# Two transformer blocks on one core: block 2's token factor moves from h to the products, and the norms' sums are issued later

## Chip, cores and metric

One core of a Trainium2 chip runs the whole kernel. The metric is the device time of one execution in microseconds (us); lower is better.

## What is computed

The input x has 512 tokens of 1024 features. It goes through a first block of two layers and then a second block of two layers. Each layer is a mixer and a feed-forward part (ffn), each with a norm ahead of it and a norm behind it. Cut to what matters here:

```python
def rms_norm_2(x, gain):
    xf = x.astype(jnp.float32)
    y = xf * lax.rsqrt(jnp.mean(xf * xf, axis=-1, keepdims=True) + RMS_EPS)
    return y.astype(x.dtype) * gain

def second_block(x, positions, ...):
    for l in range(DEPTH):
        h = rms_norm_2(x, g_pre_mix[l])
        m = hybrid_mixer_2(h, positions, w_in[l], ...)
        x = x + rms_norm_2(m, g_post_mix[l])
        h = rms_norm_2(x, g_pre_ffn[l])
        f = conv_ffn(h, w_up[l], conv_w[l], conv_b[l], w_down[l])
        x = x + rms_norm_2(f, g_post_ffn[l])
    return x
```

The first block has the same frame, but its h is `rms_norm(x) * (1 + sc) + sh`: a shift is added after the norm. In the second block the mixer begins with `h @ w_in`, which yields rotated queries and keys, values, gates and the inputs of a second attention (`sb`); the ffn is `h @ w_up`, a causal convolution over three tokens, gelu times a linear part, and `@ w_down`. In both, the reciprocal root of a token's mean square is one factor per token, so it commutes with the matrix product over features.

## The kernel before

**Layout.** Activations lie feature-major: eight tiles (KT = 8) of 128 features x 512 tokens. Every operand of a matmul is split into a high and a low part, and `mm3` (L314) makes one product of 128 features from three matmuls: hi by hi, hi by lo, lo by hi. So a tile of 128 outputs by 512 tokens takes 24 matmuls, and one over half of the tokens 24 shorter ones.

**Weights.** `load` (L257) brings a chunk by DMA into `raw`, ScalarE copies it into `whi` (L265), VectorE, or GpSimd where the caller says so, subtracts for `wlo` (L267). Four pairs of `whi` and `wlo` exist; a copy waits until TensorE has let go of a pair.

**A joint.** The last tiles of a part are made by `out_proj` (mixer) and `down2` (ffn): one tile `op` after the other, the last ones in two halves of 256 tokens by `in_halves` (L343): all items for the first half, then all in reverse order for the second. Behind the last of the first half stands the post-norm (L476: the sum of squares of y as a matmul with ones into `nrm`, then Ln and Exp for `rstd`, then for each of eight tiles `yn` at L488 and the x add at L489), and behind it the pre-norm (L437): squares of x on ScalarE (L444), adds in pairs on VectorE (L446), four matmuls into `nrm`, `rstd`, and per tile `xn` (L458), `hh` (L460, L462) and `hl` (L468, L473). `norms` (L362) says at which item of the second half each of these is issued: the post-norm at item 0, the pre-norm at item LA or LB. The second half's post-norm comes when all items are done, and its pre-norm (`pending`) is issued by `fm_split` (L377) of the next part. That makes the first tiles of the next part, over the first half of the tokens tile by tile and then over the second in reverse order; `pending` stands before the tile with number LC (ffn) or LD (mixer). The mixer makes some values (`values_steps`) between the halves.

**Order of work.** Each engine runs its instructions in the order in which a list scheduler wrote them down when the kernel was built, from the order of issue in the code and its waits; nothing is reordered when it runs, and the instruction at the head holds up what stands behind it.

**Block 2's users of h.** `mix2` takes rotated parts by `rope` (L568), copies for the compressed values (`vc`), query and key products by `sb_proj` (L1485), the merge gates by `sigmoid`, and values by `values_steps` and `ev_v`; the ffn's `conv` (L1536) reads a finished tile from its bank three times.

Of the kernel before, what the change touches and what calls it, by code (L numbers as in the profile page):

```python
# [10 lines left out]
F32 = mybir.dt.float32  # L11
# [3 lines left out]
ALU = mybir.AluOpType  # L15
# [3 lines left out]
P = 128  # L19
# [24 lines left out]
PH2 = 0  # L44
PXM = 0
SA = 0
LA = 2
# [3 lines left out]
LB = 1  # L51
LC = 4
LD = 2
# [133 lines left out]
class Net:  # L187
    def __init__(self, ctx, tc, A, out):
# [10 lines left out]
        self.pending = lambda: None  # L199
# [162 lines left out]
    def norms(self, y, sqs, g, nxt, late):  # L362
# [13 lines left out]
    def fm_split(self, chunks, act, pool, more=None):  # L376
# [60 lines left out]
    def pre_norm(self, hs, gs, sh, hh, hl):  # L437
# [4 lines left out]
        for k in range(KT):  # L442
# [6 lines left out]
            if sq is None:  # L449
                self.matmul(ps[:, :256], self.ones, s2, start=k == min(1, PAIRS), stop=k == KT - 1)  # L450
        r = self.half("rstd")
        self.ln_exp_rstd(ps[:, :256], r, D)
        ts = []
        for k in range(KT + LAG):
            if k < KT:
# [3 lines left out]
                if sh is None:  # L459
                    nc.scalar.activation(hh[k][:, hs], t, AF.Copy)  # L460
                else:
                    nc.scalar.activation(hh[k][:, hs], t, AF.Identity, bias=sh[:, k:k + 1])  # L462
            if k >= LAG:
                j = k - LAG
                lo, hi = hl[j][:, hs], hh[j][:, hs].bitcast(F32)
                pool = (PH2 if sh is None else PH1) >> j & 1
                if sh is None:
                    (nc.gpsimd if pool else nc.vector).tensor_tensor(lo, ts[j], hi, ALU.subtract)  # L468
                elif pool:
# [5 lines left out]
    def post_norm(self, hs, y, sqs, g, end=False):  # L475
# [1260 lines left out]
```

## Time and profile before

| | |
|---|---|
| median of 3 runs | 3232.23 us (3228.86 to 3241.45) |
| the profiled execution, own time | 3238.15 us |
| its span, first to last instruction | 3236.2 us |
| mean granted TensorE clock | 0.975 |
| TensorE busy | 3060.6 us (95%) |
| VectorE busy | 1958.9 us (61%) |
| ScalarE busy | 1552.1 us (48%) |

[...] A busy TensorE at half clock takes about twice as long for a matmul. A row of waits names who waited, what for, and how long altogether, how often, and at most. The seven joints lie, by the time since the start of the span, at 380 to 425 (block 1 layer 0, mixer to ffn), 755 to 830 (ffn to layer 1's mixer), 1125 to 1195 (layer 1, mixer to ffn), 1505 to 1575 (into block 2), 1975 to 2045, 2355 to 2425 and 2825 to 2885 (the same three places in block 2).

### The profile page before, as it was taken

What the parts mean: (1) busy time and instruction counts of PE and PEld (TensorE: products, weight loads), DVE (VectorE), ACT (ScalarE), POOL (GpSimd) and SP (SyncE); (2) the same over time, 40 slices, a digit from 0 to 9 for tenths busy, and PEclk for the clock granted to TensorE, in tenths of its full rate; (3) what the DMA queues carried; (4) which work ended last, traced back from release to release, by engine and by line L of the source; (5) the groups of instructions that cost most, each with busy time, mean ns of one, the idle gap of its engine ahead of it and who ended that gap; (6) DMA issues with size and microseconds to landing.
All of it is one profiled execution on the core that took longest, in us unless ns stands there. A gap on an engine that the chain in (4) does not pass through costs nothing.

```text
span 3236.2 us, 42643 instructions
## 1 busy us (share of the span) xinstructions
PE 3060.6 (95%) x16196; PEld 2552.1 (79%) x16196; DVE 1958.9 (61%) x3542; ACT 1552.1 (48%) x2768; POOL 338.4 (10%) x329
## 2 busy tenths in 40 slices
PE   6898899998999899999999998999989999999998
PEld 5674787887875688888988778888888878788887
DVE  6778575546477463235677676645566766676365
ACT  4445642234444652224477665534445866454343
POOL 4352000001442000000100111000002001200000
PEclk8899999998998999999999999999999999999999
DMA  7235365644322232323421123323243112332323
GB/s 229 82 109 197 99 215 188 214 130 149 102 89 78 72 114 83 112 86 112 150 76 40 57 68 133 115 91 104 85 158 115 40 46 72 111 118 84 112 86 107
DMA packets 118925, 358.40 MB, mean 111 GB/s; under 512 B 15408, under 2 KB 28464, under 8 KB 118720
## 3 DMA queue, kind: packets, MB, share of 16 engines
q1 hardware_dynamic: 118720, 355.68, 34.2%
q8 instruction: 127, 2.08, 0.3%
q14 instruction: 78, 0.64, 0.1%
HBM read 336.19 MB, written 8.42 MB: 106 GB/s over the span
## 4 chain that ended last, share of the span: by engine, by line
PE 69%; DVE 10%; issue 10%; ACT 5%; DMA 3%; POOL 2%; SPq 0%; POOLq 0%; DVEq 0%; ACTq 0%
PE ps L305 26%; PE op L305 12%; PE pj L305 11%; PE dn L305 7%; PE tk L305 4%; PE nrm L305 2%; PE po L305 2%; DMA wm<-in_w_mod_dram 2%; DVE wlo L267 1%; DVE yn L488 1%; PE pt L308 1%; DVE x L489 1%; POOL mg L1357 1%; ACT whi L265 1%; DVE wm L633 1%
## 5 line engine op out<-in xcount | busy, mean ns | idle before, releaser
L265 ACT ACTIVATE whi<-raw 128x1024 fp32r<-128x1024 f32 (+1 forms) x562 | 550.0, 980 | 812.1 <-PE ps L305 204.0
L267 DVE TENSOR_TENSOR wlo<-raw,whi 128x1024 fp32r<-128x1024 f32 x500 | 559.1, 1122 | 530.5 <-ACT whi L265 527.4
L305 PE MATMUL ps<-hh,whi 128*128 128x512 f32 (+1 forms) x1560 | 574.4, 368 | 0.0
L305 PE MATMUL ps<-hl,whi 128*128 128x512 f32 (+1 forms) x1560 | 572.9, 367 | 0.0
L305 PE MATMUL ps<-hh,wlo 128*128 128x512 f32 (+1 forms) x1560 | 572.7, 367 | 0.0
L305 PE MATMUL pj<-hh,whi 128*128 128x512 f32 (+1 forms) x944 | 357.0, 379 | 23.5 <-ACT hh L654 13.3
L305 PE MATMUL pj<-hl,whi 128*128 128x512 f32 (+1 forms) x944 | 354.2, 375 | 4.4 <-POOL hl L656 4.4
L305 PE MATMUL pj<-hh,wlo 128*128 128x512 f32 (+1 forms) x944 | 352.1, 373 | 0.0
L305 PEld LDWEIGHTS ps<-hh,whi 128*128 128x128 f32 x1560 | 295.4, 189 | 48.1
L305 PEld LDWEIGHTS ps<-hh,wlo 128*128 128x128 f32 x1560 | 295.2, 189 | 48.3
L305 PEld LDWEIGHTS ps<-hl,whi 128*128 128x128 f32 x1560 | 295.5, 189 | 47.9
L305 PEld LDWEIGHTS pj<-hh,whi 128*128 128x128 f32 x944 | 181.5, 193 | 65.9 <-ACT hh L654 15.7
L305 PEld LDWEIGHTS pj<-hl,whi 128*128 128x128 f32 x944 | 181.9, 193 | 35.4 <-POOL hl L656 6.6
L305 PEld LDWEIGHTS pj<-hh,wlo 128*128 128x128 f32 x944 | 181.6, 192 | 30.2 <-issue 1.0
L633 DVE CUSTOM_DVE_ANT_0 wm<-wm,cact 128x1024 f32<-128x1024 f32 x96 | 121.6, 1270 | 112.1 <-DMA wm<-in_w_mod_dram 110.2
L267 POOL TENSOR_TENSOR wlo<-raw,whi 128x1024 fp32r<-128x1024 f32 x62 | 153.5, 2491 | 285.3 <-ACT whi L265 180.2
L305 PE MATMUL op<-hidh,whi 128*128 128x256 f32 (+1 forms) x572 | 178.9, 313 | 0.0
L305 PE MATMUL op<-hidh,wlo 128*128 128x256 f32 (+1 forms) x572 | 177.4, 310 | 0.3 <-DVE wlo L267 0.3
L305 PE MATMUL op<-hidl,whi 128*128 128x256 f32 (+1 forms) x572 | 176.9, 309 | 0.0
L575 POOL TENSOR_TENSOR rp<-rp,rp 128x512 f32<-128x512 f32 (+1 forms) x20 | 28.7, 1437 | 1091.7 <-DVE rp L574 1002.5
L305 PE MATMUL dn<-hidh,whi 128*128 128x512 f32 x352 | 137.8, 391 | 2.3 <-ACT hidh L254 2.3
L305 PE MATMUL dn<-hidl,whi 128*128 128x512 f32 x352 | 137.6, 391 | 0.2 <-DVE hidl L255 0.2
(352 smaller groups left out, 6151.4 us busy)
## 6 DMA issues: line engine op xcount, KB each, us to landing
raw<-in_w_in_dram SPq DMA_DIRECT2D x134, 512.0 KB, 3.4
raw<-in_w_up_dram SPq DMA_DIRECT2D x100, 512.0 KB, 3.5
wm<-in_w_mod_dram SPq DMA_DIRECT2D x96, 512.0 KB, 4.4
raw<-in_w_gu_dram SPq DMA_DIRECT2D x94, 512.0 KB, 3.4
raw<-in_w_dn_dram SPq DMA_DIRECT2D x80, 512.0 KB, 3.5
raw<-in_w_out_dram SPq DMA_DIRECT2D x52, 512.0 KB, 3.5
raw<-in_w_dn_dram SPq DMA_DIRECT2D x80, 192.0 KB, 3.1
hp<-rp SPq DMA_DIRECT2D x96, 64.0 KB, 2.0
```

The lines of the kernel that those rows point to most:

```text
L265: nc_.scalar.activation(hi[:, :n], raw[:, :n], AF.Copy)
L267: (self.lo_eng or nc_.vector).tensor_tensor(lo[:, :n], raw[:, :n], hi[:, :n].bitcast(F32), ALU.subtract)
L305: return self.paced(self.nc.tensor.matmul(*args, **kw))
L308: return self.paced(self.nc.tensor.transpose(*args))
L488: nc.vector.scalar_tensor_tensor(t, y(k, hs), g[:, k:k + 1], r, ALU.mult, ALU.mult)
L489: (nc.gpsimd if PXM >> k & 1 else nc.vector).tensor_tensor(self.x[k][:, hs], self.x[k][:, hs], t, ALU.add)
L575: nc.gpsimd.tensor_tensor(t1[r], t1[r], t2[r], ALU.subtract)
L633: self.nc.vector.tensor_tensor_reduce(raw, raw, self.cact, 1.0, 0.0, ALU.mult, ALU.add, self.mod[l][:, c:c + 1])
L1357: nc.gpsimd.tensor_tensor(s, s, gate[1, f], ALU.add)
```

## The change

In block 2 h becomes x times the gain alone (`raw_h`). The token factor `r2` is computed beside (`token_norm`) and multiplied into what is made of the products: into the rope tables (`cosr`, `sinr`), `vc`, the gates before their sigmoid, `sb_proj`, the values by columns of r2 (`columns`, `split_by`) and each ffn tile ahead of its convolution. In both blocks the post-norm of the second half is issued inside `fm_split`, after eight products of its first tile group; the pre-norm of the first half is issued at item 4 (mixer) or 3 (ffn) instead of 2 or 1, in block 2 at the last item; the pre-norm of the second half is issued after five tiles' worth of products, in block 2's ffn later still, in a mixer between the halves. `fm_split` takes its tiles in groups of four (KG), feature tile by feature tile (`k`) across the group. The DMAs that spill x follow the second post-norm.

```diff
-LA = 2
+LA = 4
...
-LB = 1
-LC = 4
-LD = 2
+LB = 3
+LC = 5
+KG = 4
...
+    def split_by(self, src, f, hi, lo):
+
+        self.nc.scalar.activation(hi, src, AF.Copy, scale=f)
+        self.nc.vector.scalar_tensor_tensor(lo, src, f, hi.bitcast(F32), ALU.mult, ALU.subtract)
...
-        post = [lambda i=i: self.post_norm(HALVES[i], y, sqs, g) for i in range(2)]
-        pre = [lambda i=i: self.pre_norm(HALVES[i], *nxt, *h) for i in range(2)]
-        self.pending = pre[1]
-        if late == 0:
-            return {0: lambda: (post[0](), pre[0]())}, post[1], h
-        return {0: post[0], late: pre[0]}, post[1], h
+        gs, sh = nxt
+        post = [lambda i=i: self.post_norm(HALVES[i], y, sqs, g, pool=0 if sh is None else PXM) for i in range(2)]
+        if sh is None:
+            self.r2 = r2 = self.unit("r2")
+            make = [lambda i=i: self.raw_h(HALVES[i], gs, *h) for i in range(2)]
+            pre = [lambda i=i: self.token_norm(HALVES[i], r2) for i in range(2)]
+            post = [lambda i=i, p=p: (p(), make[i]()) for i, p in enumerate(post)]
+        else:
+            pre = [lambda i=i: self.pre_norm(HALVES[i], gs, sh, *h) for i in range(2)]
+        self.pending = post[1], pre[1], sh is None
+        return {0: post[0], last if sh is None else late: pre[0]}, lambda: None, h
...
-        begin = {LC if more is None else LD: self.pending}
-        middle = {} if more is None else {0: lambda: run(steps(more, 4))}
-        self.in_halves([(i, [src]) for i, src in enumerate(chunks)], KF if more is None else KM,
-                       lambda i, ws, hs, _: self.fm(tiles[i], ws[0], 0, act, hs, range(KT)), pool,
-                       begin, middle)
+        n, keep = len(chunks), KF if more is None else KM
+        late = None if more is not None else (n + 2) * KT if self.pending[2] else LC * KT
+        kept, loads, count = {}, 0, 0
+        ah, al = act
+        for hs in HALVES:
+            first = hs is HALVES[0]
+            if not first and more is not None:
+                run(steps(more, 2))
+                self.pending[1]()
+                if self.pending[2]:
+                    run(steps(more, 2))
+            order = list(range(n)) if first else list(range(n))[::-1]
+            for o in range(0, n, KG):
+                group = []
+                for i in order[o:o + KG]:
...
+                    group.append((i, ws))
+                for k in range(KT):
+                    c = slice(k * P, k * P + P)
+                    for i, (hi, lo) in group:
+                        if count == KT:
+                            self.pending[0]()
+                            if spill:
+                                self.spill()
+                        if count == late:
+                            self.pending[1]()
+                        count += 1
+                        self.mm3(tiles[i][:, hs], hi[:, c], lo[:, c], ah(k, hs), al(k, hs), k == 0, k == KT - 1)
...
+    def raw_h(self, hs, gs, hh, hl):
+
+        nc, x = self.nc, self.x
+        for k in range(KT):
+            nc.scalar.activation(hh[k][:, hs], x[k][:, hs], AF.Copy, scale=gs[:, k:k + 1])
+            nc.vector.scalar_tensor_tensor(hl[k][:, hs], x[k][:, hs], gs[:, k:k + 1], hh[k][:, hs].bitcast(F32), ALU.mult, ALU.subtract)
+
+    def token_norm(self, hs, r2):
+
+        self.ln_exp_rstd(self.squares(hs)[:, :256], r2[:, hs], D)
...
+        tabs = [self.unit(s) for s in ("cosr", "sinr")]
+        for t, o in zip(tabs, (self.cos, self.sin)):
+            nc.vector.tensor_tensor(t, o, r2, ALU.mult)
...
-            nc.scalar.activation(vc[g][0:64], pss[2 + g][64:128], AF.Copy)
-            nc.scalar.activation(vc[g][64:128, 0:T - 1], pss[2 + g][64:128, 1:T], AF.Copy)
+            nc.vector.tensor_tensor(vc[g][64:128], pss[2 + g][64:128], r2[64:128], ALU.mult)
+            nc.scalar.activation(vc[g][0:64], vc[g][64:128], AF.Copy)
+            nc.vector.tensor_tensor(vc[g][64:128, 0:T - 1], pss[2 + g][64:128, 1:T], r2[64:128, 1:T], ALU.mult)
...
-                self.sigmoid(t, ps)
+                nc.vector.tensor_tensor(t, ps, r2, ALU.mult)
+                self.sigmoid(t, t)
...
-            self.nc.scalar.activation(hi, ps, AF.Copy, scale=sc)
-            self.nc.vector.scalar_tensor_tensor(lo, ps, sc, hi.bitcast(F32), ALU.mult, ALU.subtract)
+            t = self.unit("sbt")
+            self.nc.vector.scalar_tensor_tensor(t, ps, (0.125, 1.0)[i], self.r2, ALU.mult, ALU.mult)
+            self.split(t, hi, lo)
...
-                nc.scalar.activation(c, ps, AF.Identity, bias=par[:, b:b + 1], scale=w(2))
+                nc.vector.tensor_tensor(v, ps, r2, ALU.mult)
+                nc.scalar.activation(c, v, AF.Identity, bias=par[:, b:b + 1], scale=w(2))
                 for j in (1, 0):
                     s = 2 - j
-                    nc.vector.scalar_tensor_tensor(c[:, s:], ps[:, :T - s], w(j), c[:, s:], ALU.mult, ALU.add)
+                    nc.vector.scalar_tensor_tensor(c[:, s:], v[:, :T - s], w(j), c[:, s:], ALU.mult, ALU.add)
```

How the rows of VectorE move is told by three places. The first is the joint at 380 to 425, first half: `sq` are the adds of squares that TensorE's sums wait for, `wlo` the conversions of weights. Before:

```order
L508 TENSOR_TENSOR ssy_637_3132<-ssy_637_3132,sqy_712_3498 128x256
L267 TENSOR_TENSOR wlo_745_3662<-raw_743_3660,whi_744_3661 128x1024
L508 TENSOR_TENSOR ssy_637_3132<-ssy_637_3132,sqy_714_3527 128x256
L446 TENSOR_TENSOR sq_717_3533<-sq_716_3531,sq_717_3533 128x256
L446 TENSOR_TENSOR sq_719_3539<-sq_718_3537,sq_719_3539 128x256
L446 TENSOR_TENSOR sq_721_3545<-sq_720_3543,sq_721_3545 128x256
```

And with the change, after the same `ssy` adds:

```order
L271 TENSOR_TENSOR wlo_750_3697<-raw_748_3695,whi_749_3696 128x1024
L271 TENSOR_TENSOR wlo_755_3732<-raw_753_3730,whi_754_3731 128x1024
L563 TENSOR_TENSOR ssy_637_3132<-ssy_637_3132,sqy_719_3562 128x256
L271 TENSOR_TENSOR wlo_773_3780<-raw_771_3778,whi_772_3779 128x1024
L563 TENSOR_TENSOR ssy_637_3132<-ssy_637_3132,sqy_724_3597 128x256
L490 TENSOR_TENSOR sq_727_3603<-sq_726_3601,sq_727_3603 128x256
L490 TENSOR_TENSOR sq_729_3609<-sq_728_3607,sq_729_3609 128x256
```

The adds of squares stand two tiles later, behind three more conversions, the last of them that of a weight of the next part.

The second place is the joint at 1125 to 1195, where the rope tables of block 2 (`ang`, `n`, `r`) are computed beside the post-norm's second half (`yn`). Before:

```order
L508 TENSOR_TENSOR ssy_1878_9742<-ssy_1878_9742,sqy_1988_10302 128x256
L508 TENSOR_TENSOR ssy_1878_9742<-ssy_1878_9742,sqy_1993_10337 128x256
L267 TENSOR_TENSOR wlo_2041_10539<-raw_2039_10537,whi_2040_10538 128x1024
L488 SCALAR_TENSOR_TENSOR yn_2000_10379<-y_1870_9734,mod1_122,rstd_1999_10376 128x256
L488 SCALAR_TENSOR_TENSOR yn_2001_10382<-y_1871_9735,mod1_122,rstd_1999_10376 128x256
```

With the change:

```order
L619 TENSOR_SCALAR r_2003_10385<-r_2003_10385 128x512
L614 SCALAR_TENSOR_TENSOR r_2005_10396<-n_2004_10392,ang_2001_10378 128x512
L271 TENSOR_TENSOR wlo_2044_10571<-raw_2042_10569,whi_2043_10570 128x1024
L615 SCALAR_TENSOR_TENSOR r_2005_10396<-n_2004_10392,r_2005_10396 128x512
L271 TENSOR_TENSOR wlo_2047_10577<-raw_2045_10575,whi_2046_10576 128x1024
L616 SCALAR_TENSOR_TENSOR r_2005_10396<-n_2004_10392,r_2005_10396 128x512
L271 TENSOR_TENSOR wlo_2068_10691<-raw_2066_10689,whi_2067_10690 128x1024
L618 TENSOR_SCALAR r_2005_10396<-r_2005_10396 128x512
L619 TENSOR_SCALAR r_2005_10396<-r_2005_10396 128x512
L543 SCALAR_TENSOR_TENSOR yn_2034_10473<-y_1870_9735,mod1_122,rstd_2033_10469 128x256
```

All of the tables' operations now stand ahead of `yn`, and three conversions among them.

The third place is the joint at 1975 to 2045, first half, from the last x add on. Before:

```order
L489 TENSOR_TENSOR x_3339_18085<-x_3339_18085,yn_3399_18380 128x256
L508 TENSOR_TENSOR ssy_3326_18043<-ssy_3326_18043,sqy_3401_18409 128x256
L267 TENSOR_TENSOR wlo_3434_18573<-raw_3432_18571,whi_3433_18572 128x1024
L508 TENSOR_TENSOR ssy_3326_18043<-ssy_3326_18043,sqy_3403_18438 128x256
L446 TENSOR_TENSOR sq_3406_18444<-sq_3405_18442,sq_3406_18444 128x256
```

With the change:

```order
L544 TENSOR_TENSOR x_3335_18103<-x_3335_18103,yn_3396_18399 128x256
L271 TENSOR_TENSOR wlo_3413_18548<-raw_3411_18546,whi_3412_18547 128x1024
L502 SCALAR_TENSOR_TENSOR hl_3344_18120<-x_3328_18096,par2_0_111,hh_3336_18112 128x256
L271 TENSOR_TENSOR wlo_3418_18583<-raw_3416_18581,whi_3417_18582 128x1024
L502 SCALAR_TENSOR_TENSOR hl_3345_18121<-x_3329_18097,par2_0_111,hh_3337_18113 128x256
L271 TENSOR_TENSOR wlo_3432_18645<-raw_3430_18643,whi_3431_18644 128x1024
L502 SCALAR_TENSOR_TENSOR hl_3346_18122<-x_3330_18098,par2_0_111,hh_3338_18114 128x256
```

The `hl` follow the x adds at once, conversions between them, and the squares come after.

## Rows read from the trace of the kernel before

**Rows 1.** Page, part 1: busy us of each engine, share of the span, instructions.

```profile
PE 3060.6 (95%) x16196; PEld 2552.1 (79%) x16196; DVE 1958.9 (61%) x3542; ACT 1552.1 (48%) x2768; POOL 338.4 (10%) x329
```

**Rows 2.** Stretches: length; busy us of PE, PEld, DVE, ACT, POOL; clock; DMA share; GB/s.

```profile
380.00:425.00 45.00, 41.25 (x314) 39.87 (x313) 38.59 (x82) 28.93 (x63) 0.00 (x0) 0.96 0.36 117
755.00:830.00 75.00, 59.34 (x414) 56.80 (x413) 45.64 (x87) 34.31 (x66) 22.04 (x9) 0.86 0.38 122
1125.00:1195.00 70.00, 59.10 (x431) 56.62 (x430) 51.70 (x103) 37.93 (x71) 0.00 (x0) 0.90 0.33 105
1505.00:1575.00 70.00, 61.08 (x438) 58.64 (x437) 48.26 (x102) 33.16 (x67) 0.00 (x0) 0.90 0.45 144
1975.00:2045.00 70.00, 66.09 (x514) 64.14 (x513) 47.77 (x97) 37.06 (x77) 0.00 (x0) 0.98 0.34 114
2355.00:2425.00 70.00, 61.07 (x466) 59.14 (x465) 49.53 (x104) 33.85 (x67) 0.00 (x0) 0.95 0.47 155
2825.00:2885.00 60.00, 56.25 (x431) 54.35 (x431) 43.33 (x92) 33.12 (x71) 0.00 (x0) 0.97 0.32 106
1575.00:1975.00 400.00, 385.83 (x2112) 319.54 (x2111) 268.47 (x562) 255.87 (x548) 50.77 (x73) 0.99 0.24 77
2045.00:2355.00 310.00, 310.00 (x1452) 260.28 (x1452) 171.51 (x215) 130.25 (x174) 0.00 (x0) 1.00 0.31 99
```

**Rows 3.** TensorE's waits by joint: 380:425 (as 2825), 755:830 (two), 1125, 1505 (as 2355), 1975.

```profile
PE nrm L305 <- DVE sq L446: 3.7, 1, 3.7
...
PE nrm L305 <- DVE sq L446: 11.9, 2, 6.1
...
PE nrm L305 <- DVE ssy L1087: 3.8, 1, 3.8
...
PE nrm L305 <- DVE sq L446: 10.9, 2, 7.1
...
PE nrm L305 <- DVE sq L446: 8.9, 2, 5.8
...
PE nrm L305 <- DVE sq L446: 3.9, 2, 3.7
```

**Rows 4.** TensorE's waits from 1575 to 1975, the mixer's products.

```profile
PE pj L305 <- DVE mg L1324: 3.1, 5, 1.2
...
PE pj L305 <- ACT mg L275: 1.8, 1, 1.8
```

**Rows 5.** VectorE in order of time: start, us, operation, idle before.

```profile
1983.94 0.88 DVE L488 SCALAR_TENSOR_TENSOR yn<-y,par,rstd 128x256 f32<-128x256 f32 x2 [4.17 <-ACT rstd L275]
...
1989.13 0.76 DVE L489 TENSOR_TENSOR x<-x,yn 128x256 f32<-128x256 f32 x2
...
1996.44 1.67 DVE L458 SCALAR_TENSOR_TENSOR xn<-x,par,rstd 128x256 f32<-128x256 f32 x4 [2.27 <-ACT rstd L275]
```

**Rows 6.** Groups by line: a weight's copy (1560 to 2045) and its conversion (2045 to 2355).

```profile
L265 ACT ACTIVATE whi<-raw 128x1024 fp32r<-128x1024 f32 x65 | 68.6, 1056 | 59.7 <-PE pj L305 28.4 <-PE op L305 13.1 <-PE ps L305 11.3
...
L267 DVE TENSOR_TENSOR wlo<-raw,whi 128x1024 fp32r<-128x1024 f32 x53 | 65.0, 1226 | 109.9 <-ACT whi L265 109.9
```

**Rows 7.** GpSimd's conversions from 755 to 830, and VectorE at 797.39.

```profile
L267 POOL TENSOR_TENSOR wlo<-raw,whi 128x1024 fp32r<-128x1024 f32 x9 | 22.1, 2487 | 131.0 <-PE op L305 104.9 <-ACT whi L265 26.0
...
797.39 2.99 DVE L488 SCALAR_TENSOR_TENSOR yn<-y,mod,rstd 128x256 f32<-128x256 f32 x2
```

**Rows 8.** VectorE in order of time, from 1125 to 1200.

```profile
1161.02 0.43 DVE L551 CAST ang<-pi 128x512 f32<-128x512 int32 x1
...
1171.16 0.42 DVE L446 TENSOR_TENSOR sq<-sq,sq 128x256 f32<-128x256 f32 x1
```

**Rows 9.** Groups by line: a rope product out of a bank, 1560 to 2045.

```profile
L573 DVE TENSOR_TENSOR rp<-pj,cos 128x512 f32<-128x512 f32 x3 | 2.1, 687 | 4.2 <-PE pj L305 4.2
```

**Rows 10.** TensorE in order of time: two matmuls over 256 tokens in a row.

```profile
1126.15 0.28 PE L305 MATMUL op<-ch,whi 128*128 128x256 f32 x1
1126.27 0.28 PE L305 MATMUL op<-cl,whi 128*128 128x256 f32 x1
```

More of the change, by code (lines that the diff above doesn't have):

```diff
@@ L360, in in_halves, with norms @@
             items = items[::-1]
-    def norms(self, y, sqs, g, nxt, late):
+    def norms(self, y, sqs, g, nxt, late, last):
         if nxt is None:
@@ new lines, in norms, with fm_split @@
+        self.pending = post[1], pre[1], sh is None
+        return {0: post[0], last if sh is None else late: pre[0]}, lambda: None, h
+    def fm_split(self, chunks, act, pool, more=None, spill=False):
+        tiles = [self.ps("pj" if i < PJ else "ps") for i, _ in enumerate(chunks)]
+        n, keep = len(chunks), KF if more is None else KM
[13 more added lines that the diff above has]
+                for i in order[o:o + KG]:
+                    ws = kept.pop(i, None)
+                    if ws is None:
+                        old = self.lo_eng
+                        if pool >> loads & 1:
+                            self.lo_eng = self.nc.gpsimd
+                        loads += 1
+                        ws = self.load(chunks[i])
+                        self.lo_eng = old
+                    if first and i >= n - keep:
+                        kept[i] = ws
+                    group.append((i, ws))
[10 more added lines that the diff above has]
+                        self.mm3(tiles[i][:, hs], hi[:, c], lo[:, c], ah(k, hs), al(k, hs), k == 0, k == KT - 1)
+        if more is not None and not self.pending[2]:
+            run(steps(more, 2))
@@ L513, in out_proj @@
         self.unspill()
-        middle, end, h = self.norms(y, (ss, last), g, nxt, LA)
+        middle, end, h = self.norms(y, (ss, last), g, nxt, LA, ntail - 1)
         self.in_halves([(f, [src for _, src in chunks(f)]) for f in range(KT - ntail, KT)], KO, one, pool, {}, middle)
@@ L686, in mix1 @@
         self.lo_eng = nc.gpsimd if LO1 else None
-        self.spill()
         self.mark("1.split")
@@ L710, in mix1 @@
             more = seq(*vms)
-            pss = self.fm_split([W[0], W[1], W[2]], act, PS1, more)
+            pss = self.fm_split([W[0], W[1], W[2]], act, PS1, more, spill=True)
             run(more)
         else:
+            self.spill()
             pss, tps = self.fm_fed([W[0], W[1], W[2]], [(range(4), W[23]), (range(4, 8), W[24])], 256, act, feed)
@@ L935, in values_tiles, with columns, col, values_steps @@
         return [self.unit("vh", F32R) for _ in range(NB)], [self.unit("vl", F32R) for _ in range(NB)]
-    def values_steps(self, v, chunks, act):
+    def columns(self):
+        c = self.sp.tile([P, 2 * NB], F32, tag="r2c", bufs=2, name=self.nm("r2c"))
+        have = set()
+        def col(t, negated=False):
+            if t // 2 not in have:
+                have.add(t // 2)
+                ps, s = self.ps("rt"), t // 2 * 2
+                for j in range(2):
+                    self.transpose(ps[:, j * P:j * P + P], self.r2[:, (s + j) * P:(s + j) * P + P], self.ident)
+                v = ps[:, 0:256].rearrange("p (a b) -> p a b", a=2)[:, :, 0]
+                self.nc.vector.tensor_copy(c[:, s:s + 2], v)
+                self.nc.vector.tensor_scalar(c[:, NB + s:NB + s + 2], v, -1.0, None, ALU.mult)
+            i = t + NB * negated
+            return c[:, i:i + 1]
+        return col
+    def values_steps(self, v, chunks, act, col):
         for i, (a, b) in enumerate(chunks):
@@ L1091, in down2 @@
         self.use(LN_EXP)
-        middle, end, h = self.norms(lambda k, cs: y[k][:, cs], (ss, last), g, nxt, LB)
+        middle, end, h = self.norms(lambda k, cs: y[k][:, cs], (ss, last), g, nxt, LB, ntail - 1)
         self.in_halves([(f, [src for _, src in chunks(f)]) for f in range(KT - ntail, KT)], KD, one, pool, {}, middle)
@@ L1206, in ev_v @@
             hi, lo = (vv[i][t // 2][:, (t % 2) * 256:(t % 2) * 256 + 256] for i in range(2))
[L1207 to L1208 removed]
+            self.split_by(ps[:, 0:256], cols(t), hi, lo)
+            self.act(gates[:, t, :], ps[:, 256:280], AF.Exp, scale=cols(t, True))
         def values():
```

55 lines of the change are left out of this document (25 added, 30 removed).

## The prediction

> **What bounds the kernel.** I read the engine table first: TensorE is busy 3060.6 of 3236.2 us, VectorE 1958.9 [rows 1]. Then the table by stretches: the long stretches between two parts are nearly full (block 2's ffn 310.00 of 310 us at clock 1.00, its mixer 385.83 of 400 at 0.99), while the seven stretches in which one part hands over to the next are short of work and of clock [rows 2]. Then what TensorE waits for there: `nrm<-sq`, the norm's sums, until VectorE has added the squares; 51.9 us in the seven stretches (8.9 and 3.7 stand for two of them each), and 3.8 for `nrm<-ssy`, 55.7 together [rows 3]. The clock's loss by [rows 2] is (1 − clock) × length: 1.8, 10.5, 7.0, 7.0, 1.4, 3.5 and 1.8, together 33.0 us. So the joints hold at most 55.7 + 33.0 = 88.7 us, and nothing else that this change touches costs TensorE much: in a mixer of block 2 the tiles of the gates and of `sb` cost it 3.1 and 1.8 us [rows 4]. Why the waits: the post-norm's sixteen products and adds run from 1983.94 to 1989.89, then come squares, their adds, the sum, `rstd`, and only at 1996.44 the first `xn` [rows 5].
>
> **The change, part by part.** In block 2 h no longer needs `rstd`: after the x adds follow `hh` (ScalarE) and `hl` (VectorE), and the twelve or so us from 1983.94 to 1996.44 shrink to six. TensorE does the squares at the last tail tile, so that sum delays nothing but r2, which is wanted with the first finished tile. In block 1 the chain stays and only moves.
>
> *Joint 380 to 425 (block 1, into the ffn).* The squares are summed two tiles later, but the order shows a conversion, `wlo_773`, in front of their adds, whose copy waits for a buffer that the tile just before the sums gives back. So the adds start one copy (1.06, [rows 6]) and one conversion (1.23, [rows 6]) after that tile and need four steps more: about 3.1 us of wait in place of 3.7. Four tiles that go k by k give back their buffers together, and the next group's first low half comes a conversion late: about 1 us. Together +0.4; bounds −5.5 (wait 3.7 and clock 1.8 gone) and +2.
>
> *Joint 755 to 830 (block 1, into its second mixer).* Of the waits 6.1, 5.8 and 3.8 the first half's falls to 3.1 as above (−2.7); `ssy` now has eight products' cover, so its 3.8 falls to 1.5 (−2.3); the rest stays. −5.0. GpSimd converts weights here at 2487 ns each, and two of VectorE's `yn` took 2.99 us while it did [rows 7], against 0.88 [rows 5]. In the new order three such conversions are wanted at once, by the first four tiles. [...] By the rows that is at most 3 × 2.5 = 7.5 us; so the bounds are −15.7 (all three waits) and +7.5.
>
> *Joint 1125 to 1195 (block 1, into its second ffn).* The rope tables for block 2, seventeen VectorE operations that begin at 1161.02 [rows 8], stood behind the post-norm's second half and now stand before it, with three weight conversions among them that wait for copies whose buffers come free only at the end of the first group of four, about 1159. From there the conversions and the last table operations take until about 1168, the post-norm 6 us to 1174, the squares until 1176; before, the last square was added at 1171.6 [rows 8]. Four and a half us later, with 0.7 won at the first half and about 1.2 us more of other tiles ahead of the second: +2.6. Bounds: 0 (tables finish before the buffers matter) and +6.
>
> *Joint 1505 to 1575 (into block 2).* It loses 8.9 to waits [rows 3] and 7.0 to clock [rows 2], 15.9. I leave 0.8 (square adds behind one conversion), 2.3 (the last `hl`, which alternate with conversions of 1.23) and 1.2 (edge of the group), 4.3, and 2.6 of clock: 9.0 won. r2 costs about 1.0 before the first values leave. After the four tiles two tables are multiplied and four pieces of `vc` taken, 6 × 0.69 [rows 9] = 4.1 us on VectorE ahead of the compress products; with the rope products, copies and conversions that stand there already I count some 14 us of VectorE against 92 products of the values × 0.12 [rows 10] = 11 us, so a wait of 2.5 that wasn't there. Net −5.5; bounds −15.9 and 0.
>
> *Joint 2355 to 2425 (into the second mixer).* The same with 8.9 + 3.5 = 12.4 to begin with: 12.4 − 4.3 − 2.4 − 1.0 − 2.5 = 2.2. Bounds −12.4 and +3.
>
> *Joints 1975 to 2045 and 2825 to 2885 (mixer into ffn, block 2).* They lose 5.3 and 5.5; 0.8 at the sums and 1.0 at the group's edge stay: −3.5 each, −7.0; bounds −11 and 0.
>
> *Block 2's ffn.* 44 products more per layer, at 0.69 [rows 9] 30 us, on a VectorE that is busy 171.51 of 310 while TensorE never waits [rows 2]: 201 of 310, hidden. ScalarE's first step of the convolution starts one product later, but the bank is free after a single read. If the cover were gone, 30 us per layer would show. Moving the DMAs that spill x behind the first products costs nothing: SP only issues, and x isn't read again until the part's end.
>
> *Block 2's mixer.* Sixteen gate tiles and eight `sb` tiles per layer now leave their bank by an in-order VectorE product instead of a ScalarE read. The nearest rows: sixteen `mg` tiles a layer that leave so already cost TensorE 3.1 us, 0.19 each; the gates and `sb` tiles, 24 by ScalarE, 1.8, 0.08 each [rows 4]. So 48 × 0.11 = 5.3 us at most and 0 at least, where those waits only take the place of others; I take the middle, +2.7. The 32 values tiles split by column factors cost as before.
>
> **Sum:** 0.4 − 5.0 + 2.6 − 5.5 − 2.2 − 7.0 + 2.7 = −14.0 us. The profiled execution took 3238.15 us, 5.9 above the median of the three runs, 3232.23. 3238.2 − 14.0 = 3224.2 there, 3218 as a median.
>
> **Rivals.** *The joints close, clock and all.* Block 2's four joints hold 15.9 + 5.3 + 12.4 + 5.5 = 39.1 us; if their new waits vanish, and block 1's joints give 5 while the bodies cost 2, the gain is 42: 3190. For it: six us of cover are won and the wait was 5.8 at most. Against it: conversions keep standing in front of the `hl`. The clock stood at 0.90 over the joint with waits up to 7.1, and at 0.99 in the mixer, where TensorE waits 14 us as well, in pieces [rows 2, 3]. [...]
>
> *Waits only change names* (the change doesn't do what it says): weights are converted on VectorE in order, and what h no longer waits for, the first products wait for as `wlo` or `hl`. The joint 380 to 425 shows it already in the order. Time 3232, give or take 6.
>
> *Slower: in-order evictions.* There are few banks for `pj`. If each of the 48 gate and `sb` tiles stands behind a conversion (1.23), TensorE loses up to 59 us. It decides from (16 + 14)/48 = 0.62 us per tile on; at 0.75 it costs 36 against 14 won, 3254. For it: VectorE carries 268 of 400 us there [rows 2] and gets some 18 more. Against it: 0.19 per tile on the tiles that already leave so.
>
> **How the numbers follow.** 0.5%, about 16 us, is what a measurement here can tell from no change: below 3216 is faster, above 3248 slower. My forecast 3218 with its bounds (3206 to 3230, the larger terms not all at one end) has 0.48, of it 0.21 below 3216 and 0.27 above; the closed joints 0.21, all faster; waits that change names 0.18, all same; the evictions 0.10, slower; the rope tables and GpSimd both at their upper ends (+3.4 and +12.5 against the sum, about even) with evictions in part 0.03, slower. So 0.42, 0.45 and 0.13. For 8 in 10 the range runs from 3192, which leaves out half of the closed joints, to 3240, which leaves out the evictions.
>
> **What the changed profile should show.** Right: in the four joints of block 2 the wait `nrm<-sq` below 1 us and clock at 0.95 or more; in the joint 1125 to 1195 a wait of some 9 us until `sq` again, after the table operations; 3 us still at 380 to 425; a wait of `cmp` in both mixers; the ffn of block 2 still full with VectorE at 65%. Wrong: `pj` waiting for `mg` or `sbt` over 15 us in a mixer (evictions); waits on `hl` or `wlo` of over 4 us at each joint (changed names); any wait inside the ffn of block 2.

## The result, and the profile after

The changed kernel takes 3251.03 us (median; 3247.6 to 3254.21), before 3232.23: ratio 1.0052, 95% interval 1.0035 to 1.0069. It is slower by 0.5%, just over the bound of 3248 us that the prediction set for telling it from no change; forecast were 3218 and a range up to 3240. The profiled execution took 3249.86 us, its span is 3248.1, 11.9 more than before. The medians lie 18.8 us apart; the traces show less of it, since the profiled execution before was 5.9 us above its median and this one is 1.2 below.

The page's engine table of the changed kernel answers to [rows 1]; VectorE has 70 us more, TensorE 8.6:

```profile
PE 3069.2 (94%) x16204; PEld 2555.4 (79%) x16204; DVE 2028.8 (62%) x3634; ACT 1562.4 (48%) x2764; POOL 341.6 (11%) x329
```

To see where the 11.9 us come from, the span is cut at the first matmul of each run of tiles `op` (a part's last tiles), `dn` (an ffn's first down tiles) and `sc` (the first attention of block 2), whose starts the trace gives. Of the cuts left out (`dn` to `op`, 179.52 twice, and the end behind the last `op`, 75.3) none changed.

| from, to | what lies in it | before | after | difference | forecast |
|---|---|---|---|---|---|
| start to op | first mixer | 347.75 | 348.58 | +0.8 | 0 |
| op to op | joint 380, ffn | 364.39 | 364.56 | +0.2 | +0.4 |
| op to op | joint 755, mixer | 380.32 | 377.21 | −3.1 | −5.0 |
| op to dn | joint 1125, ffn | 191.04 | 195.13 | +4.1 | +2.6 |
| op to sc | joint 1505 | 176.33 | 170.16 | −6.2 | −5.5 |
| **sc to op** | **mixer, block 2** | **312.85** | **324.85** | **+12.0** | **+1.35** |
| op to dn | joint 1975, ffn | 182.45 | 180.06 | −2.4 | −3.5 |
| op to sc | joint 2355 | 172.30 | 168.40 | −3.9 | −2.2 |
| **sc to op** | **mixer, block 2** | **312.59** | **325.19** | **+12.6** | **+1.35** |
| op to op | joint 2825, ffn | 361.81 | 359.65 | −2.2 | −3.5 |

The seven joints gave −13.5 where −16.7 was forecast. The mixers of block 2 gave +24.6 where +2.7 was. The table by stretches of the changed kernel (length; busy us of PE, PEld, DVE, ACT, POOL; clock, as a share of full speed) shows both, to be held against [rows 2]; the stretches are shifted a little, as the parts are:

```profile
755.00:830.00 75.00, 61.15 (x419) 56.91 (x418) 48.54 (x88) 32.48 (x64) 20.29 (x9) 0.91 0.38 125
1120.00:1195.00 75.00, 60.41 (x438) 57.52 (x438) 52.69 (x108) 38.16 (x72) 0.00 (x0) 0.89 0.23 78
1505.00:1575.00 70.00, 66.76 (x506) 64.30 (x506) 45.65 (x95) 35.38 (x69) 0.00 (x0) 0.98 0.46 157
1980.00:2050.00 70.00, 69.10 (x545) 67.11 (x545) 43.70 (x83) 39.63 (x82) 0.00 (x0) 1.00 0.35 113
2360.00:2425.00 65.00, 61.98 (x479) 59.50 (x478) 45.06 (x94) 33.86 (x67) 0.00 (x0) 1.00 0.47 161
2055.00:2365.00 310.00, 310.00 (x1454) 260.36 (x1454) 197.77 (x260) 132.87 (x175) 0.00 (x0) 1.00 0.31 99
```

Into block 2 TensorE is now busy 66.76 of 70 us at clock 0.98 instead of 61.08 at 0.90. Block 2's ffn is full, and its 44 more products are hidden (VectorE 197.77 of 310, 64%). At 1125 it got worse, 0.89.

The mixer, from the first `sc` to the first `op`, before:

```profile
1639.35:1952.20 312.85, 302.14 (x1538) 242.81 (x1538) 217.74 (x476) 218.27 (x478) 34.70 (x61) 0.99 0.17 55
```

and after:

```profile
1635.15:1960.00 324.85, 306.42 (x1538) 246.08 (x1538) 232.03 (x500) 219.18 (x478) 38.10 (x61) 0.97 0.16 53
```

The same 1538 matmuls: 4.3 us more busy at a lower clock, 0.97 in place of 0.99, and 12.0 − 4.3 = 7.7 us more idle. VectorE has 24 instructions and 14.3 us more, the 16 gate products and 8 `sb` products. What TensorE waits for in this stretch (total us, times, longest), the longest row before and four rows after:

```profile
PE pt L308 <- ACT ss L275: 3.4, 2, 2.6
```

```profile
PE pt L312 <- ACT ss L279: 5.2, 3, 3.1
PE pj L309 <- DVE mg L1394: 4.2, 3, 3.0
PE pj L309 <- DVE sbt L1574: 4.0, 1, 4.0
PE pj L309 <- DVE mg L1405: 3.1, 5, 1.2
```

Two of these are the new products, L1394 (a gate) and L1574 (`sb`); the last, L1405, are tiles that left by VectorE before too (3.1 us then as well, [rows 4]). Of the 24 products one gate makes TensorE wait 3.0 us and one `sb` 4.0, two more gates 1.2 together, the others none. VectorE's rows at the two places say why, in order of time (start, us, operation, idle before):

```profile
1661.48 1.23 DVE L271 TENSOR_TENSOR wlo<-raw,whi 128x1024 fp32r<-128x1024 f32 x1 [1.31 <-ACT whi L269]
...
1662.82 0.67 DVE L1394 TENSOR_TENSOR mg<-pj,r 128x512 f32<-128x512 f32 x1
...
1820.61 1.27 DVE L1561 TENSOR_TENSOR_SCAN ss<-sa 128x128 f32<-128x128 f32 x2 [0.51 <-POOL sa L1559]
1821.80 0.67 DVE L1574 SCALAR_TENSOR_TENSOR sbt<-pj,r 128x512 f32<-128x512 f32 x1
```

and TensorE's there:

```profile
1663.55 0.50 PE L309 MATMUL pj<-hh,whi 128*128 128x512 f32 x1 [2.97 <-DVE mg L1394]
...
1822.52 0.80 PE L309 MATMUL pj<-hh,whi 128*128 128x512 f32 x1 [3.95 <-DVE sbt L1574]
```

The gate's product stands in VectorE's order behind a weight conversion that itself waits for its copy (1.31 us); the `sb` product stands behind the scans of the previous pair, which wait 0.51 us for GpSimd, and what GpSimd works on there was made on VectorE after 1.57 us of waiting for ScalarE. Before, TensorE waited at the second place too, 1.8 us [rows 4], until ScalarE had read a gate tile, and went on at 1818.49. The bank of the `sb` tile was free no earlier then: VectorE's `sbl` also reads it, and stood behind the scans already. Before's ScalarE and VectorE there:

```profile
1817.85 0.59 ACT L275 ACTIVATE mg<-pj 128x512 f32<-128x512 f32 x1
```

```profile
1819.89 0.67 DVE L1494 SCALAR_TENSOR_TENSOR sbl<-pj,sbh 128x512 fp32r<-128x512 f32 x1
```

So what the change took away at the second place is the early read of the gate tile. That is the reading; the runs below test it.

### The profile page after: what moved, and what is told of

The parts are those of the page before. It is cut to its first block, busy times and chain, and to the rows that moved or that the text cites. A ratio compares the mean times of both kernels' runs of the same rounds, so it can differ in the third digit from the quotient of the medians.

```text
span 3248.1 us, 42774 instructions
## 1 busy us (share of the span) xinstructions
PE 3069.2 (94%) x16204; PEld 2555.4 (79%) x16204; DVE 2028.8 (62%) x3634; ACT 1562.4 (48%) x2764; POOL 341.6 (11%) x329
## 4 chain that ended last, share of the span: by engine, by line
PE 69%; issue 10%; DVE 10%; ACT 5%; POOL 2%; DMA 2%; SPq 0%; POOLq 0%; DVEq 0%; ACTq 0%
PE ps L309 28%; PE op L309 12%; PE pj L309 10%; PE dn L309 7%; PE tk L309 4%; PE po L309 3%; PE nrm L309 2%; DVE wlo L271 1%; PE pt L312 1%; DVE ss L1561 1%; ACT whi L269 1%; DVE yn L543 1%; POOL mg L1438 1%; DVE x L544 1%; DVE sa L1558 1%
## 5 line engine op out<-in xcount | busy, mean ns | idle before, releaser
L309 PE MATMUL pj<-hh,whi 128*128 128x512 f32 (+1 forms) x944 | 359.5, 381 | 36.4 <-ACT hh L710 12.6
```

What stands on the lines that cost most here:

```text
L309: return self.paced(self.nc.tensor.matmul(*args, **kw))
```

## The experiments

Three theories at the start. Theory 1: the 24 tiles hold their banks until VectorE gets to them in order. Theory 2: VectorE's added work makes a path through it longer, whoever frees the bank. Theory 3: the products have nothing to do with it; the new order of everything in the mixer does. Mixer lengths are from the first `sc` to the first `op` of the first of the two mixers; before 312.85, with the change 324.85.

### ScalarE or GpSimd in VectorE's place

Edit of `scalar_then_vector` in the gates; in `sb` the same, with its scale; the other has `gpsimd` in the third line:

```diff
-                nc.vector.tensor_tensor(t, ps, r2, ALU.mult)
+                nc.scalar.activation(t, ps, AF.Copy)
+                nc.vector.tensor_tensor(t, t, r2, ALU.mult)
```

> ScalarE copies a gate or sb tile out of its bank, VectorE multiplies the copy by the token factor in SBUF: the same VectorE work as in the changed kernel (0.69 us each), 24 copies of 0.58 us more per layer on ScalarE, the bank free as early as before. Theory 1: most of the loss comes back, 3230 to 3236 us, no pj wait on sbt or on a gate product. Theory 2: nothing comes back, 3249 to 3256, since VectorE has the same to do and ScalarE more. Theory 3: 3249 or more.

> As the run before, but GpSimd multiplies the copy (its 128x512 product of two SBUF operands takes 1.44 us, the rope rows show), so VectorE does as little as before the change. Theory 1: as the run before, 3230 to 3238. Theory 2: the loss comes back here and not there, 3230 to 3238 against 3249 or more. Theory 3: 3249 or more.

Measured: 3258.58 us (ratio 1.0071, 1.0056 to 1.0086) and 3292.56 us (1.0175, 1.0157 to 1.0194). Mixers 328.13 and 341.96. With VectorE behind ScalarE's copy, the longest wait on an `sb` tile fell from 4.0 to 1.3 us, and instead `pt` waits 6.5 us at a time on `ss`:

```profile
PE pt L312 <- ACT ss L279: 7.1, 2, 6.5
...
PE pj L309 <- ACT mg L1394: 4.7, 3, 2.0
```

With GpSimd the groups by line show 1.5 us for each product (that engine's rows):

```profile
L1395 POOL TENSOR_TENSOR mg<-mg,r 128x512 f32<-128x512 f32 x16 | 24.1, 1507 | 84.0 <-ACT mg L1394 68.3 <-PE pt L312 15.7
```

So a bank freed earlier, at the price of 24 more ScalarE reads in a mixer, brings nothing back: what is added goes into an order that `sb`'s own chain needs, ScalarE's as well as VectorE's. Theory 1 as it was put (3230 to 3238) falls, though these runs add work and so don't test the bank by itself; which of 2 and 3 holds was left.

### Neither product, or one of them

In place of the token factor stands a constant 0.2, applied by ScalarE while it reads the bank as before. So the factor is left out of the computation: of gates and `sb` queries and keys (`no_factor`), of `sb` alone, of the gates alone.

```diff
-            self.nc.vector.scalar_tensor_tensor(t, ps, (0.125, 1.0)[i], self.r2, ALU.mult, ALU.mult)
-            self.split(t, hi, lo)
+            sc = (0.125 * 0.2, 0.2)[i]
+            self.nc.scalar.activation(hi, ps, AF.Copy, scale=sc)
+            self.nc.vector.scalar_tensor_tensor(lo, ps, sc, hi.bitcast(F32), ALU.mult, ALU.subtract)
...
-                nc.vector.tensor_tensor(t, ps, r2, ALU.mult)
-                self.sigmoid(t, t)
+                self.act(t, ps, AF.Exp, scale=-0.2)
+                self.act(t, t, AF.Ln, bias=1.0)
+                self.act(t, t, AF.Exp, scale=-1.0)
```

> The changed kernel with the gates and the sb queries and keys leaving their banks by ScalarE as before; in place of the token factor stands a constant 0.2, so that product is left out of the computation (16 gate tiles and 8 sb tiles per layer of block 2). The copies by ScalarE before VectorE's products brought nothing back (3258.6), so an early free bank is not what is missing. Theory 2, VectorE's added work: between the end of the sc matmuls and the end of the sz matmuls VectorE got 16 more products, 16 x 0.69 = 11.0 us, and the stretch grew by 10.7 and 11.2 us, so the stretch is bound by the path through VectorE. Then about 3228 us here, the stretch back at 148 us. Theory 3, the new order of everything in the mixer: 3249 or more, the stretch stays 158 us. Theory 1 (banks held): 3228 as well, but its other run spoke against it.

> The same for the eight sb tiles per layer alone (a constant 0.2 in place of the token factor there). Theory 2: 8 x 0.69 = 5.5 us per layer come back, about 3240. Theory 3: 3249 or more. If the sb tiles alone make the loss, since they stand at the head of each pair's path and the gates beside it: 3229.

> The same for the sixteen gate tiles per layer alone; eight of them are made between sc and sz, eight earlier, where the stretch grew by 1.3 us. Theory 2: 5.5 + 1.3 us per layer come back, about 3237. Theory 3: 3249 or more. If the sb tiles alone make the loss: 3248.

Measured: 3224.78 us (0.9972, 0.9957 to 0.9987), 3252.72 (1.0056, 1.0038 to 1.0074) and 3247.28 (1.0043, 1.0027 to 1.0058). The mixer's stretch without both products:

```profile
1634.37:1947.02 312.65, 301.71 (x1539) 242.60 (x1539) 217.53 (x476) 218.16 (x478) 34.79 (x61) 0.99 0.17 55
```

without the `sb` products alone:

```profile
1634.88:1956.38 321.50, 303.50 (x1539) 242.64 (x1538) 227.19 (x492) 217.64 (x478) 36.82 (x61) 0.99 0.17 54
```

without the gates' alone:

```profile
1639.70:1960.33 320.63, 303.68 (x1538) 243.87 (x1538) 223.27 (x484) 218.08 (x478) 36.02 (x61) 0.98 0.16 54
```

Without both, all 12.2 us come back, and the kernel is 0.3% faster than before: theory 3 falls. But the two parts don't add: gates alone cost 321.50 − 312.65 = 8.9 us, `sb` alone 8.0, both 12.2 (in the second mixer 8.9, 9.1 and 12.3). A sum over instructions (theory 2: 5.5 of 11.0 for `sb`) doesn't give that; either kind alone makes most of the loss. The medians say so more strongly: without the `sb` products nothing came back, without the gates' 4 us (the trace without the `sb` products is of an execution 9.8 us below its median).

The rows at the second place say why. Without the `sb` products the wait of some 4 us stays, on VectorE's other read of the same bank:

```profile
PE pj L309 <- DVE sbl L1575: 4.8, 2, 4.1
```

Without the gates' products it stays as well (`sbt`, 3.9 us), since ScalarE's read of the gate tile now stands behind a copy that waits for the `sb` product:

```profile
1820.93 0.63 ACT L253 ACTIVATE sbh<-sbt 128x512 fp32r<-128x512 f32 x1 [3.18 <-DVE sbt L1575]
1821.47 0.58 ACT L279 ACTIVATE mg<-pj 128x512 f32<-128x512 f32 x1
```

Either kind alone takes away the early read of the gate tile, so by these rows the loss at this place is in both runs and counts once when the two are together.

### The products alone, in the kernel before

```diff
+        self.one512 = self.cp.tile([P, T], F32, name="one512")
+        nc.vector.memset(self.one512, 1.0)
...
-                self.sigmoid(t, ps)
+                nc.vector.tensor_tensor(t, ps, self.one512, ALU.mult)
+                self.sigmoid(t, t)
```

and the same in `sb_proj`. The tile holds ones, and a product with ones changes no value.

> The kernel before with nothing but this: its gate tiles (16 per mixer of block 2) and sb tiles (8) leave their banks by a VectorE product with a tile of ones, as they do with the change by the product with the token factor. Theory A, an in-order product in two wrong places: one alone of the two kinds of product brought nothing back, both together 26 us, so a product delays TensorE where it stands in VectorE's order behind an operation that waits (a conversion, the scan of the sb weights), and the clock falls behind it. Then the part alone costs what it costs in the changed kernel, 20 to 28 us: 3252 to 3260, each mixer some 12 us longer, between sc and the end of sz. Theory B, the loss comes from the raw h or the new order together with the products: 3232 to 3242.

Measured: 3254.92 us (1.0070, 1.0055 to 1.0085), so 23 us for the products alone (with them, in `sb`, goes ScalarE's copy, which now reads the product and not the bank). The mixer and its waits:

```profile
1632.39:1956.44 324.05, 305.04 (x1538) 244.90 (x1538) 232.11 (x500) 219.07 (x478) 37.43 (x61) 0.98 0.16 53
```

```profile
PE pj L307 <- DVE mg L1316: 4.1, 3, 3.0
PE pj L307 <- DVE sbt L1496: 4.1, 1, 4.1
```

The same two waits, 3.0 and 4.1 us, without any of the rest of the change. Theory A holds against B: the loss is the products'. Whether it is their place or their amount on VectorE (theory 2) this run can't tell; that the parts don't add speaks for the place.

### A third bank, an earlier projection, conversions on GpSimd

Three edits of one line each in the changed kernel:

```diff
-PJ = 2
+PJ = 3
```
```diff
-            pt.append(Task(sb_proj(pr), 3, s0 + d * (pr - 1), s0 + d * pr))
+            pt.append(Task(sb_proj(pr), 3, s0 + d * (pr - 1.5), s0 + d * (pr - 0.5)))
```
```diff
-LO2 = 0
+LO2 = 1
```

> The changed kernel with three banks for pj and five for all else in place of two and six. Theory A1: what TensorE waits for at 1660 (3.0 us) and 1818 (4.0 us) is a free bank; with a third both waits are gone or under 1 us, and each stretch between sc and the end of sz gets 6 to 12 us shorter, unless five banks for the rest bring waits of their own there. Theory A2: the bank is not what is missing, as the copies by ScalarE suggested: the same waits in other names (pt on ss) and the stretch within 2 us of the changed kernel's. Together with the other parts, where six banks are used by the early tiles, 3235 to 3255.

> The changed kernel with the sb projections of each pair due half a pair earlier, so that most of their products stand ahead of the previous pair's scans in VectorE's order, not between a scan and what follows. Theory A: the wait of 4.0 us of pj on sbt and the half clock behind it go, 4 to 8 us less per mixer, 3236 to 3245; the wait of 3.0 us on a gate product stays. If VectorE's amount of work bounds the stretch: no change, 3247 to 3253.

> The changed kernel with the weight conversions of block 2's mixers on GpSimd in place of VectorE (94 of them, about 2.5 us each there, two mixers). In VectorE's rows the gate product that TensorE waits 3.0 us for stands behind a conversion that waits for its copy. If it is that conversion that holds it, the wait of 3.0 goes and the stretch from the first sc matmul to the first sz matmul gets 3 to 5 us shorter than the 138.7 of the changed kernel; the wait of 4.0 on the sb product behind the scans stays. Against it GpSimd's own rows beside VectorE's two-operand ones: products of VectorE that meet them take longer, and the conversions come later, so the whole can be 3240 to 3270.

Measured: 3254.42 us (1.0072, 1.0057 to 1.0087), 3255.51 (1.0074, 1.0059 to 1.0089) and 3281.94 (1.0146, 1.0133 to 1.0159).

With three banks the mixer is 4.5 us shorter:

```profile
1634.55:1954.93 320.38, 303.78 (x1538) 245.81 (x1538) 230.52 (x499) 219.10 (x477) 34.81 (x60) 0.98 0.17 53
```

The gate's wait is gone and the one on `sb` (4.3 us) stays. But the 4.5 us aren't won where the loss is: from the first `sc` to the last `sz` matmul the mixer takes 278.4 us, with the change 278.3, before 266.3, and what is shorter is the part behind, 42.0 us in place of 46.5 both before and after. So a third bank gives nothing back there, which is nearer to A2. (From the last `sc` to the last `sz` the stretch is 4.3 us shorter, and the `sc` matmuls take 4.3 more.) The joints into the ffn got 8 us longer each (perhaps because their early tiles have only five other banks; not tested), so the kernel gains nothing. With the projections earlier the expectation failed: the wait on `sb` stays and gates wait more, the mixer has 327.83 us:

```profile
PE pj L309 <- DVE mg L1394: 9.2, 3, 4.9
...
PE pj L309 <- DVE sbt L1574: 3.9, 1, 3.9
```

With the conversions off VectorE the longest wait on a gate fell from 3.0 to 1.7 us, but the waits on gates add up to 4.1, as with the change (4.2). The `sb` wait stays at 4.0, `pt` waits 8.0 on `ss`, and the first `sz` comes 140.6 us after the first `sc`, where 3 to 5 less than 138.7 were expected. VectorE's `sbl` made of `sbt`, eight in the first mixer, took 1.24 us each here and 0.74 with the change; the gate products took 0.68 in both. The mixers take 332.90 and 327.68 us, and the joint before the first 11 us more than with the change:

```profile
PE pt L312 <- ACT ss L279: 8.0, 3, 4.7
PE pj L309 <- DVE mg L1394: 4.1, 4, 1.7
PE pj L309 <- DVE sbt L1574: 4.0, 1, 4.0
```

So the conversion was at most a part of what held up that gate's product, and the expectation failed. No move of one piece repaired the stretch: the waits shift to the next thing in order. That the two places make the loss is read from the rows; no run gave it back by mending them.

### The rope tables at the joint 1125

```diff
+                if l == 1 and f == 5:
+                    self.rope_tables(A["positions_2"])
                 return t
 
-            if l == 1:
-                self.rope_tables(A["positions_2"])
```

> The changed kernel with the rope tables of block 2 computed inside block 1's last ffn, after its sixth pair of tiles, instead of ahead of it. The theory that the tables' 17 operations hold up the post-norm at the joint 1125 to 1195: the wait of 7.9 us of nrm on the squares falls to 0 to 3, the clock there from 0.89 to 0.95 or more, and the kernel becomes 7 to 12 us faster, 3239 to 3244. If instead the three conversions among them hold it up, the wait stays at 5 us or more, and 3247 to 3251 is measured.

Measured: 3238.87 us (1.0019, 1.0009 to 1.0028), 12 us faster than the changed kernel; the stretch from `op` to `dn` takes 182.63 us, with the change 195.13, before 191.04. In the changed kernel ScalarE's rows at the joint are

```profile
1161.91 0.63 ACT L279 ACTIVATE cos<-r 128x512 f32<-128x512 f32 x1 [3.14 <-DVE r L619]
1162.55 1.28 ACT L292 ACT_TABLE_LOAD   x1
1163.84 0.47 ACT L279 ACTIVATE rstd<-nrm,eps 128x256 f32<-128x256 f32 x1
```

and VectorE's

```profile
1161.45 0.43 DVE L619 TENSOR_SCALAR r<-r 128x512 f32<-128x512 f32 x1
1164.80 0.88 DVE L543 SCALAR_TENSOR_TENSOR yn<-y,mod,rstd 128x256 f32<-128x256 f32 x2 [2.92 <-ACT rstd L279]
```

The post-norm's `rstd` stands on ScalarE behind the last table and a load of function tables (0.63 and 1.28 us), so `yn` waits 2.92 us more after the tables' operations. VectorE's rows ran there as the listing of this joint with the change has them: from `r` of L619, at 1155.41, to `yn`, at 1164.80, the ten stand in the same order. TensorE waits 7.9 us for the squares, until 1171.12:

```profile
PE nrm L309 <- DVE sq L490: 10.9, 2, 7.9
```

The granted clock is 0.50 over the 17.1 us from 1165.9, the end of that wait among them:

```profile
1165.90:1183.00 17.10, 9.04 (x32) 7.79 (x33) 12.60 (x34) 8.72 (x19) 0.00 (x0) 0.50 0.00 1
```

Within it, from 1178.6 to 1182.8, a matmul over 256 tokens started every 0.21 us; from 1183.1 to 1186, at 1.00, every 0.12.

With the tables later that wait is gone (the 3.0 of the first half stays), and the clock over the joint is 0.98:

```profile
1120.00:1195.00 75.00, 70.54 (x512) 66.55 (x511) 50.37 (x98) 40.10 (x78) 0.00 (x0) 0.98 0.34 112
```

### A version that beats both

The raw h for block 2's ffn alone: its mixers take a normalized h again, so none of the mixer's products are needed, and the tables are later. In the second run the joints into the mixers are issued as before the change as well (the lines from `if mix and sh is None` on; the others are in both runs).

```diff
-        if sh is None:
+        raw = sh is None and not mix
+        if raw:
...
+        if mix and sh is None:
+            self.pending = None, pre[1], False
+            return {0: post[0], 1: pre[0]}, post[1], h
...
-        middle, end, h = self.norms(lambda k, cs: y[k][:, cs], (ss, last), g, nxt, LB, ntail - 1)
+        middle, end, h = self.norms(lambda k, cs: y[k][:, cs], (ss, last), g, nxt, LB, ntail - 1, mix=True)
```

> The changed kernel with the raw h and the token factor kept for block 2's ffn alone (its mixers take a normalized h as before, with the new places of the norms), and the rope tables inside block 1's last ffn. By the stretches measured: mixers 12.1 and 12.6 us shorter than in the changed kernel, joints into the ffn 2.4 to 3.7 us better than before as they were, the joints into the mixers between what they are with the change (6.2 and 3.9 better than before) and nothing, the tables 12. Sum 3214 to 3224, faster than both kernels. If the mixers' loss doesn't come from the products, 3236 to 3245.

> As the run with the raw h in block 2's ffn alone and later tables (3224.3), but the joints into block 2's two mixers are issued as before the change (second post-norm at the end of the part, pre-norms one item and two tiles in, tile by tile). With the new order and a normalized h those two joints, up to the first sc matmul, took 177.4 and 177.1 us; before 176.3 and 172.3; with the raw h 170.2 and 168.4. If the new order by itself is no gain there without the raw h, 5.9 us come back: 3216 to 3221. If the longer times were from the tables' new place or from chance, 3222 to 3227.

Measured: 3224.26 us (0.9972, 0.9963 to 0.9982) and 3224.31 (0.9965, 0.9953 to 0.9978): faster than both kernels, and not to be told from each other. The median of the second run missed the 3216 to 3221 that were expected if the new order without the raw h is a loss there, and lies in the range of the other theory, chance or the tables. The traces speak for a loss: the joints 1505 and 2355 take 177.44 and 177.12 us in the first run, 173.78 and 172.42 in the second, 8.4 us less, and at 2355 the three traces with the old order lie at 172.26 to 172.42. But the trace of the first run is of the slowest of its ten executions (3231.62 us), so the loss is likely and not shown.

## Why the prediction was wrong

**The step that failed** is the term "Block 2's mixer", +2.7 us ("48 × 0.11 = 5.3 us at most and 0 at least ... I take the middle"). It measured +24.6 (+23 alone, in the kernel before), more than four times its upper bound. The bound came from the mean of `mg` tiles that already left by VectorE, 0.19 us each [rows 4]. Those stand late in the mixer, from 1883.9 to 1956.2; VectorE isn't freer there (busy 50.12 of the 74 us from 1883, 68%; 70% from 1639 to 1883), but the mean says nothing of what stands ahead of the other 24. The price isn't one per tile: two of 24 tiles stand behind an operation that waits, and TensorE waits 3.0 and 4.0 us there and 1.2 at two more; the wait of `pt` on `ss` grows by 1.8 (from 3.4 before), and the same matmuls take 4.3 us more at the lower clock. The old wait on ScalarE's gates, 1.8, goes. The term also took the eight `sb` tiles for ones that leave by ScalarE: before, VectorE's `sbl` read their banks as well, and it was ScalarE's read of a gate tile that let TensorE go on early. The rival "in-order evictions" had the mechanism, conversions in front of a product, a price of 0.5 us per tile would have met it (24.6/48), and it had a chance of 0.10. A mean spoke against it, where the order of VectorE and the trace of before show at least the scans ahead of `sbl`. Its sign was set badly too: over 15 us of `pj` waits on `mg` or `sbt` in a mixer was asked; 11.3 were measured, 3.1 of them there before, and clock and `ss` made up the rest.

**Right in sign and near in size:** the joints. 380 to 425: forecast 3.1 us of wait where 3.7 was, measured 3.0:

```profile
PE nrm L309 <- DVE sq L490: 3.0, 1, 3.0
```

Into block 2 −6.2 and −3.9 (forecast −5.5 and −2.2); the waits `nrm<-sq` are gone there and no wait of `cmp` came, so that part of the sum, 2.5 each, was too dark, and the rest of it too bright, by 1.8 and 0.8. Mixer into ffn −2.4 and −2.2 (−3.5 each). The ffn of block 2 stayed full, as said.

**The joint 1125** was forecast at +2.6 and was +4.1 in that stretch; the mechanism was half right. The three conversions among the tables' operations were done by 1161.08, on time; the tables held up the post-norm through ScalarE, whose `rstd` stood behind `cos` and a table load, a queue that the prediction didn't walk. It put the tables' end at about 1168; it came at 1161.88. Two errors the opposite way brought it near, a wait of some 9 us foretold and 7.9 measured; that is luck. Moving the tables took 12.5 us off, 8.4 below before: what the tables' place cost was more than the rest of the new order gained there.

**The joint 755** gave −3.1 of −5.0, by other parts than foretold. Of the 15.7 us of waits for the norm's sums [rows 3] 4.4 stayed, so more was won there than the 5.0 of the sum; but new waits came, 9.4 us in all, 5.3 of them for GpSimd's conversions:

```profile
PE nrm L309 <- DVE sq L490: 4.4, 2, 2.9
PE ps L309 <- ACT hh L520: 2.1, 1, 2.1
PE ps L309 <- POOL wlo L271: 1.9, 1, 1.9
PE tk L309 <- POOL wlo L271: 1.8, 1, 1.8
PE pj L309 <- POOL wlo L271: 1.6, 2, 1.2
```

That is, in this joint, the rival "waits only change names". GpSimd's conversions again stood beside `yn`, as these rows of GpSimd and of VectorE show:

```profile
800.27 5.39 POOL L271 TENSOR_TENSOR wlo<-raw,whi 128x1024 fp32r<-128x1024 f32 x2 [8.90 <-ACT whi L269]
```

```profile
800.84 5.10 DVE L543 SCALAR_TENSOR_TENSOR yn<-y,mod,rstd 128x256 f32<-128x256 f32 x2
```

Two `yn` took 5.10 us, nearly as long as GpSimd's two conversions, 5.39; the two before them, at 799.38 with GpSimd idle, took 0.88. Here that cost 5.10 − 0.88 = 4.2 us of VectorE's time, within the 7.5 that was kept as a bound, an estimate from the length of three conversions [rows 7]. The rows show the times and not the cause. It isn't what is missing at this joint, though, for it cost as much before: the two `yn` of 2.99 us [rows 7] and the two x adds behind them,

```profile
800.31 2.90 DVE L489 TENSOR_TENSOR x<-x,yn 128x256 f32<-128x256 f32 x2
```

where such pairs take 0.88 and 0.76 us [rows 5] with GpSimd idle (0.00 us from 1975 to 2045, [rows 2]), 4.3 us more together.

The rival in which the joints close altogether didn't come, since block 1's keep their waits; but block 2's nearly did: 1980 to 2050 is busy 69.10 of 70 at clock 1.00.

## What to carry to other kernels

The price of moving a bank's eviction to another engine was not a mean over like instructions here: look in the order at what stands directly ahead of each one, whether that waits, and which read of a bank comes first today. Here two places of 24 hold 7.0 of the 8.2 us that TensorE waits for the new products. Products that were hidden in one part (44 per ffn, whose stretch stays full) cost 12 us in another (24 per mixer) where the same engine carries a chain of its own, so keep an algebraic trick where its cover is. Walk every queue that a moved block passes, ScalarE's table loads too (1.28 us at the joint 1125).

## What was not expected of the hardware

Beside a long wait the clock was low too: around the end of the wait of 7.9 us at 1171 the granted clock was 0.50 for 17.1 us, of which TensorE was busy 9.04; in a mixer 4.3 of 12.0 us are slower matmuls. And the stretches of block 1 are not the same from trace to trace even where their code is: from the second to the third run of `op` tiles the changed kernel took 377.21 us, its variants 372.65 to 381.02, while in block 2 unchanged stretches agree within 0.4 us (312.59 to 312.95 for eight mixers without the products). With the products the same mixer varies more, 322.58 to 325.19 us in four (two of the changed kernel, two with the tables later). As there is one trace of each kernel, kernel and execution can't be told apart here. Differences of under 5 us between medians were therefore read from block 2's stretches.
